# Closings of 14 row tiles: the residual rows added by an accumulating transfer, the post factor joined to the row factor

## The chip, the cores and the metric

One core of one Trainium2 chip runs the whole program. The metric is the device time of one execution in microseconds (us), the median of three executions. Engines are named as in the profile: PE (matmuls), DVE (VectorE), ACT (ScalarE), POOL (GpSimd), SP (the queue that issues most transfers).

## The reference

One decoder layer is applied to a prompt of 2048 rows and to a sample group of 32 rows. Four mixers (convolution, pooling, stick-breaking attention, cross-attention) give `mix`, 2048 values a row. What matters here is the end of the layer:

```python
out = rms_norm(mix @ w_out, post_g)     # y * rsqrt(mean(y*y) + eps) * post_g
xp = x + out
y_prompt = rms_norm(xp, final_g)
```

So every output row needs two row factors in turn: one from the sum of squares of the projection, one from the sum of squares of residual plus normalised projection. All of it is float32.

## The kernel before, in words

The program first does the input projections and the sample group's attention, then the prompt's attention, and at last the output projection `mix @ w_out`. That projection works on 16 row tiles of 128 rows and two halves of 512 columns. It is written as seven products for each pair of row tiles i (0 to 7), which are then combined by additions in two kept buffers, `U2` and `U3`. Products 1, 7, 2 and 6 run first, for all i. From position `last_` of the list `order` (L1915 to L1919) products 4, 5 and 3 follow, in the order (4,0) (4,1) (5,0) (5,1) (4,2) (5,2) (3,0) (3,1) (3,2), then the sample rows (5,8) (3,8), then for i = 3 to 7 each (4,i) (5,i) (3,i). This document calls that part the last stage. A product is 24 matmuls of 128x512 into one PSUM bank (tile `acc`). The eight banks are taken in turn: three of pool `accp`, five of `accp2` (L1962).

When a product is complete, `out_ready` adds the kept buffers to it on DVE (L1768, L1769), ACT takes its sum of squares (L1729, into `ssk`), DVE multiplies it by its half of `post_g` (L1772, in place in the bank), and the bank is held. Product 5 completes row tile t = 2i + 1, product 3 row tile t = 2i. The first half of an even tile was computed earlier and stored to DRAM; it comes back as tile `oh` (L1784), and POOL multiplies it by `post_g` (L1788, `out_factor`).

A complete row tile is closed by `out_tile`. The residual rows are loaded into tile `oxt` by SP (L1794; three buffers). DVE adds the two partial sums of squares (L1798), ACT takes the root (L1799), DVE the reciprocal (L1800). DVE then does one instruction per half, `xt = half * factor + xt` (L1804), and ACT squares each half with a sum (L1805). DVE, ACT and DVE make the second factor (L1808, L1809, L1810), DVE multiplies by it and by `final_g` (L1815), and SP stores the rows (L1817). The small tile `oss` that holds these factors has one buffer, so a closing begins only when the closing before it has done L1815. Tile 14 uses the other half of tile 15's buffer, so these two overlap.

PE runs in the order of the code. For DVE, ACT, POOL and SP a scheduler that works at build time chooses the order, and each of them then executes its list strictly in order. What feeds the last stage shares these lists: SP loads the rows of `mix` (`mr`, L1672, L1687), POOL adds two of them for product 5 (L1699), ACT rounds them (`mh`, L1714), DVE takes the remainder (`ml`, L1725), and PE multiplies (L1969).

Of the kernel before, what the change touches and what calls it, by code (L numbers as in the profile page):

```python
# [13 lines left out]
ALU = mybir.AluOpType  # L14
# [4 lines left out]
P = 128  # L19
# [68 lines left out]
def kernel(  # L88
# [9 lines left out]
    pe, act, dve, pool, sp = nc.tensor, nc.scalar, nc.vector, nc.gpsimd, nc.sync  # L98
    wq = nc.sync

    xp, xs = x_prompt[0], x_sample.rearrange("b t d -> (b t) d")
# [1625 lines left out]
    def square(c, t, half):  # L1727
        rows = P if t < 16 else NS
        act.activation(out=junk[:rows], in_=c[:rows], func=AF.Square, accum_out=ssk[:rows, t, half : half + 1])  # L1729

    def out_ready(prod, i, o):

        if i == LAST:
            if prod == 5:
                return
            both = (ope.tile([P, 512], F32, tag="oh", name="both3", bufs=OH) if prod == 3 else
                    op.tile([P, 512], F32, name=f"both{prod}", bufs=1))
            act.copy(both[:NS], o[NS : 2 * NS])
            dve.tensor_tensor(out=both[:NS], in0=both[:NS], in1=o[:NS], op=ALU.add)
            if prod == 1:  # L1740
                keep["s"] = both
            elif prod == 2:
                dve.tensor_tensor(out=both[:NS], in0=both[:NS], in1=keep["s"][:NS], op=ALU.add)
                square(both, 16, 0)
                keep[16, 0] = both
            else:
                dve.tensor_tensor(out=o[:NS], in0=both[:NS], in1=keep["s"][:NS], op=ALU.add)
                square(o, 16, 1)
                dve.tensor_tensor(out=o[:NS], in0=o[:NS], in1=gpost[:NS, 512:], op=ALU.mult)
                dve.tensor_tensor(out=keep[16, 0][:NS], in0=keep[16, 0][:NS], in1=gpost[:NS, :512], op=ALU.mult)  # L1750
                out_tile(16, keep[16, 0], o)
            return
        t = 2 * i + (prod in (4, 5))
        if prod == 1:
            act.copy(U2[:, i], o)
        elif prod == 7:
            dve.tensor_tensor(out=U3[:, i], in0=o, in1=U2[:, i], op=ALU.add)
        elif prod == 6:
            dve.tensor_tensor(out=U3[:, i], in0=o, in1=U3[:, i], op=ALU.add)
            dve.tensor_tensor(out=U2[:, i], in0=o, in1=U2[:, i], op=ALU.add)  # L1760
        elif prod == 2:
            c = opw.tile([P, 512], F32, tag="c11", name=f"c11_{i}", bufs=1)
            dve.tensor_tensor(out=c, in0=o, in1=U2[:, i], op=ALU.add)
            square(c, t, 0)
            sp.dma_start(c11d[i], c)
        else:
            if prod == 5:
                dve.tensor_tensor(out=U2[:, i], in0=o, in1=U2[:, i], op=ALU.add)  # L1768
            dve.tensor_tensor(out=o, in0=o, in1=(U2 if prod == 3 else U3)[:, i], op=ALU.add)  # L1769
            half = 0 if prod == 4 else 1  # L1770
            square(o, t, half)
            dve.tensor_tensor(out=o, in0=o, in1=gpost[:, 512 * half : 512 * half + 512], op=ALU.mult)  # L1772
            keep[t, half] = o
            if prod != 4:
                out_tile(t, keep[t, 0], keep[t, 1])
            if (prod, i) == (3, 0):
                out_first(2)
            if prod == 5 and i != 2 or (prod, i) == (3, 1):
                out_factor(2 if prod == 3 else i)

    def out_first(i):

        c = ope.tile([P, 512], F32, tag="oh", name=f"oh2_{i}", bufs=OH)
        sp.dma_start(c, c11d[i])  # L1784
        keep[2 * i, 0] = c

    def out_factor(i):
        pool.tensor_tensor(out=keep[2 * i, 0], in0=keep[2 * i, 0], in1=gpost[:, :512], op=ALU.mult)  # L1788

    def out_tile(t, a, b):  # L1790

        rows = P if t < 16 else NS
        xt = ope.tile([P, D], F32, tag="oxt", name=f"oxt{t}", bufs=OX)[:rows]
        sp.dma_start(xt, xp[P * t : P * t + P, :] if t < 16 else xs)  # L1794
        if t != 14:
            keep["ss"] = ope.tile([P, 6], F32, tag="oss", name=f"oss{t}", bufs=1)
        ss = keep["ss"][:rows, 3:] if t == 14 else keep["ss"][:rows]
        dve.tensor_tensor(out=ss[:, 0:1], in0=ssk[:rows, t, 0:1], in1=ssk[:rows, t, 1:2], op=ALU.add)  # L1798
        act.activation(out=ss[:, 0:1], in_=ss[:, 0:1], func=AF.Sqrt, bias=eps_t[:rows], scale=1.0 / D)  # L1799
        dve.reciprocal(out=ss[:, 0:1], in_=ss[:, 0:1])  # L1800
        last = t == 14
        halves = (slice(0, 512), slice(512, 1024))
        for n, (hs, src) in enumerate(zip(halves, (a[:rows], b[:rows]))):
            dve.scalar_tensor_tensor(out=xt[:, hs], in0=src, scalar=ss[:, 0:1], in1=xt[:, hs], op0=ALU.mult, op1=ALU.add)  # L1804
            act.activation(out=junk[:rows], in_=xt[:, hs], func=AF.Square, accum_out=ss[:, n + 1 : n + 2])  # L1805
        if last:
            keep.pop("end")()
        dve.tensor_tensor(out=ss[:, 1:2], in0=ss[:, 1:2], in1=ss[:, 2:3], op=ALU.add)  # L1808
        act.activation(out=ss[:, 1:2], in_=ss[:, 1:2], func=AF.Sqrt, bias=eps_t[:rows], scale=1.0 / D)  # L1809
        dve.reciprocal(out=ss[:, 1:2], in_=ss[:, 1:2])  # L1810
        dst = y_prompt[0, P * t : P * t + P, :] if t < 16 else y_sample.rearrange("b t d -> (b t) d")

        def end():
            for n, hs in enumerate(halves if last else (slice(0, 1024),)):
                dve.scalar_tensor_tensor(out=xt[:, hs], in0=xt[:, hs], scalar=ss[:, 1:2], in1=gfin[:rows, hs],  # L1815
                                         op0=ALU.mult, op1=ALU.mult)
                (wq if n else sp).dma_start(dst[:, hs], xt[:, hs])  # L1817

        if t == 15:
            keep["end"] = end  # L1820
        else:
            end()
# [186 lines left out]
    op = oy.enter_context(tc.tile_pool(name="op", bufs=1, side="right", reuse_waits="tile"))  # L2009
# [74 lines left out]
    for n, x in enumerate(parts):  # L2084
        if n == last_:
# [3 lines left out]
            gpost = ope.tile([P, D], F32, name="gpost", bufs=1)  # L2089
# [3 lines left out]
        prod, i, h = x  # L2093
# [20 lines left out]
        while done:  # L2114
            out_ready(*done.pop(0))
# [33 lines left out]
```

## Time and profile before

| | us |
|---|---|
| median of 3 executions | 2368.04 (2366.82 to 2369.79) |
| the profiled execution, its own time | 2371.25 |
| its span in the trace | 2369.5 |
| last stage, from its first loads to the last matmul | about 2212 to 2354.5 |
| from the last matmul to the end of the span | 15.0 |
| busy over the span: PE, DVE, ACT, POOL | 96%, 72%, 47%, 54% |

Rows of the timeline give start (us from the start of the span), duration (us), engine, line, operation, output and inputs. Rows that group instructions give the count behind an x and durations in ns. SPq is the issuing side of SP's queue; an issue is not the transfer, which goes on after it.

### The profile page before, as it was taken

The numbers are of one execution on the slowest core, as the hardware profiler recorded it, in microseconds if no ns is written. First come the engines' busy times: TensorE is split into PE (matmuls) and PEld (weight loads), VectorE is DVE, ScalarE is ACT, GpSimd is POOL, SyncE is SP. The second block draws the span as 40 slices with busy tenths as digits, with TensorE's granted clock in tenths as the row PEclk, the third lists the DMA queues.
The fourth block names the chain that finished last, engine by engine and source line by source line (L and its number), as shares of the span: only waits on it lengthen the run. The fifth ranks groups of instructions, "written<-read, shape, count | busy, mean of one in ns | idle before, by whom it ended". The sixth has DMA issues, their size and how long they took to land. (4 is left out here: it accounts for less than half of the span.)

```text
span 2369.5 us, 42238 instructions
## 1 busy us (share of the span) xinstructions
PE 2280.5 (96%) x16024; PEld 1775.3 (75%) x16024; DVE 1716.2 (72%) x2428; ACT 1117.2 (47%) x1947; POOL 1273.2 (54%) x1322
## 2 busy tenths in 40 slices
PE   7999999999999999999999999899999999989997
PEld 7998888898888777777777777555555557778775
DVE  5332696969747664577787868888897956777897
ACT  5322243242442322234242324798989965444554
POOL 3554545556474645545546463688988754432230
PEclk9999999999999999999999999999999999999998
DMA  6688977878778999987877775756534207766774
GB/s 206 198 268 282 344 270 258 287 251 287 245 261 313 308 356 332 328 282 263 303 265 257 275 268 151 175 167 173 164 115 114 76 26 248 260 207 200 237 247 150
DMA packets 336868, 557.94 MB, mean 235 GB/s; under 512 B 27985, under 2 KB 212433, under 8 KB 320266
## 3 DMA queue, kind: packets, MB, share of 16 engines
q1 hardware_dynamic: 281290, 286.53, 39.1%
q0 software_dynamic: 55376, 268.72, 32.1%
q8 instruction: 126, 2.06, 0.3%
q14 instruction: 76, 0.62, 0.1%
HBM read 465.09 MB, written 90.68 MB: 235 GB/s over the span
## 5 line engine op out<-in xcount | busy, mean ns | idle before, releaser
L966 DVE STREAM_TRANSPOSE T<-kt 128x1024 f32<-128x1024 f32 x256 | 308.6, 1226 | 192.5 <-PE sSA L979 178.9
L933 POOL DMA_INDIRECT vt<-in_cache_v_dram,idv x256 | 252.4, 986 | 257.1 <-PE sO L1018 196.0
L618 DVE SCALAR_TENSOR_TENSOR cacc<-U,par,cacc 128x512 f32<-128x512 f32 x480 | 359.7, 749 | 11.0
L1344 POOL TENSOR_TENSOR be<-be,E 128x512 f32<-128x512 f32 (+3 forms) x316 | 299.9, 961 | 59.8 <-DVE E L1335 25.8
L1335 DVE TENSOR_TENSOR_SCAN E<-gam,cr,ZM 128x513 f32<-128x513 f32 x192 | 232.7, 1262 | 14.6 <-ACT gam L1266 11.2
L933 POOL DMA_INDIRECT kt<-in_cache_k_dram,idk x128 | 128.1, 1001 | 197.3 <-DVE T L966 150.2
L1355 PEld LDWEIGHTS AT<-ident,be 128*128 128x128 f32 x1082 | 116.1, 141 | 128.9 <-ACT at L1361 48.2
L1969 PE MATMUL acc<-wohi,mh 128*128 128x512 f32 (+1 forms) x480 | 194.7, 406 | 1.6 <-ACT mh L1714 1.0
L1266 ACT ACTIVATE gam<-S,nbias_bc 128x1024 f32<-128x1024 f32 (+1 forms) x158 | 172.9, 1094 | 42.6 <-ACT be L1267 18.6
L1969 PE MATMUL acc<-wolo,mh 128*128 128x512 f32 (+1 forms) x480 | 190.8, 397 | 0.0
L1969 PE MATMUL acc<-wohi,ml 128*128 128x512 f32 x448 | 179.3, 400 | 8.1 <-DVE ml L1725 8.1
L1262 PE MATMUL S<-kT,Q 128*128 128x512 f32 (+1 forms) x632 | 173.5, 397 | 4.9 <-ACT be L1267 4.8
L1267 ACT ACTIVATE be<-S,bias_bc 128x1024 f32<-128x1024 f32 (+1 forms) x158 | 171.7, 1087 | 0.9 <-DMA gsd<-sg1sg 0.9
L1355 PE MATMUL AT<-ident,be 128*128 128x128 f32 x1082 | 157.5, 283 | 13.9 <-DVE at L1359 7.4
L1371 PE MATMUL av<-at,V 128*64 128x512 f32 (+3 forms) x640 | 152.8, 556 | 3.5 <-DVE sbo L1376 3.5
L979 PE MATMUL sSA<-T,W 128*32 128x128 f32 x4096 | 140.5, 276 | 3.3 <-DVE T L966 1.4
L979 PEld LDWEIGHTS sSA<-T,W 128*32 128x32 f32 x4096 | 105.3, 109 | 38.5 <-issue 31.5
L1018 PE MATMUL sO<-vt,saT 128*32 128x512 f32 x1024 | 122.1, 592 | 0.0
L1262 PEld LDWEIGHTS S<-kT,Q 128*128 128x128 f32 x632 | 104.5, 192 | 18.5 <-ACT be L1267 6.3
L1361 ACT COPY at<-AT 128x512 f32<-128x512 f32 x192 | 110.9, 677 | 12.2 <-PE AT L1355 12.2
L1332 DVE TENSOR_TENSOR_SCAN E<-gam,ZM 128x384 f32<-128x384 f32 (+1 forms) x124 | 94.3, 809 | 28.6 <-ACT gam L1266 23.5
L1725 DVE TENSOR_TENSOR ml<-mr,mh 128x512 fp32r<-128x512 f32 x108 | 86.6, 808 | 33.5 <-ACT mh L1714 33.3
(577 smaller groups left out, 6036.2 us busy)
## 6 DMA issues: line engine op xcount, KB each, us to landing
Q<-qd SPq DMA_DIRECT2D x64, 256.0 KB
mr<-mixd SPq DMA_DIRECT2D x32, 512.0 KB
mr<-mixd SPq DMA_DIRECT2D x48, 256.0 KB
xtp<-in_x_prompt_dram SPq DMA_DIRECT2D x16, 512.0 KB
kT<-kd SPq DMA_DIRECT2D x64, 128.0 KB
ws<-in_w_out_dram SPq DMA_DIRECT2D x16, 512.0 KB
wsd<-ws SPq DMA_DIRECT2D x16, 512.0 KB
msd<-mr SPq DMA_DIRECT2D x32, 256.0 KB
```

Source lines behind the costliest of these rows:

```text
L618: dve.scalar_tensor_tensor(out=ps, in0=U[:, a + k : a + k + H], scalar=wd[:, k : k + 1], in1=ps, op0=ALU.mult, op1=ALU.add)
L933: pool.indirect_dma_start(out=dst, out_offset=None, in_=rows, in_offset=bass.IndirectOffsetOnAxis(ap=idx, axis=0))
L966: S["turn"] = dve.transpose(T[:, 2 * hh : 2 * hh + 2].rearrange("p s j t -> p (s j t)"), kt[:, 2 * hh : 2 * hh + 2].rearrange("p s j d -> ...
L979: pe.matmul(sSs[n][32 * g : 32 * g + 32, P * ml : P * (ml + 1)], lhsT=W[:, jj, :], rhs=T[:, :, jj, :], start=i == 0, stop=i == 3, tile_pos ...
L1262: pe.matmul(S[:, j, :w], lhsT=Q[:, x, P * (q2 + j) : P * (q2 + j + 1)], rhs=kt[:, :w], start=x == 0, stop=x == 1)
L1266: act.activation(out=ga, in_=S[:, :, :w], func=AF.Sigmoid, bias=nbias_bc[:, h : h + 1], scale=-1.0)
L1267: act.activation(out=be, in_=S[:, :, :w], func=AF.Sigmoid, bias=bias_bc[:, h : h + 1])
L1335: dve.tensor_tensor_scan(out=E[:, j][:, ::-1], data0=g_[:, j][:, ::-1], data1=ZM[:, 0:1].to_broadcast([P, 513]), initial=carry[hh, q2][:, ...
L1344: newest.append(pool.tensor_tensor(out=be[:, j, :m], in0=be[:, j, :m], in1=E[:, j, 513 - w : 513 - w + m], op=ALU.mult).ins)
L1355: pe.transpose(ap_[:, P * qt : P * (qt + 1)], A[hp, qb, kc, hh, qt][:, P * r : P * (r + 1)], ident)
L1371: pe.matmul(av[64 * hh : 64 * hh + 64, c], lhsT=V[:, 4 * kc + r, 64 * hh : 64 * hh + 64], rhs=ats.pop((hp, qb, kc, r, hh))[:, c], start=dg ...
L1969: pe.matmul(o[:rows], lhsT=m[a][:, k, :rows], rhs=W[prod, 4 * h + k][w], start=not cont and h == k == n == 0, stop=h == 1 and k == 3 and n ...
```

## The change

For the 14 row tiles t = 0 to 13:

- L1772 (multiplication of a finished half by `post_g` on DVE) and L1788 (the same for `oh` on POOL) are left out. Only the three halves of tiles 14 and 15 that pass L1772, and the one L1788 for tile 14, remain.
- L1804 becomes `xt = half * factor * post_g`, which writes `oxt` and no longer reads it (L1811 in the changed kernel).
- The load of the residual rows by SP goes away. In its place POOL issues a transfer that reads the same rows from DRAM and adds them to `oxt` (L1814). It waits for both L1811, and both squares of ACT (now L1816) wait for it.

Tiles 14, 15 and the sample tile 16 are closed as before.

```diff
@@ out_ready
             square(o, t, half)
-            dve.tensor_tensor(out=o, in0=o, in1=gpost[:, 512 * half : 512 * half + 512], op=ALU.mult)
+            if t > 13:
+                dve.tensor_tensor(out=o, in0=o, in1=gpost[:, 512 * half : 512 * half + 512], op=ALU.mult)
             keep[t, half] = o
...
-            if prod == 5 and i != 2 or (prod, i) == (3, 1):
-                out_factor(2 if prod == 3 else i)
+            if (prod, i) == (5, 7):
+                out_factor(i)
@@ out_tile
-        sp.dma_start(xt, xp[P * t : P * t + P, :] if t < 16 else xs)
+        x_rows = xp[P * t : P * t + P, :] if t < 16 else xs
+        if t > 13:
+            sp.dma_start(xt, x_rows)
...
-        for n, (hs, src) in enumerate(zip(halves, (a[:rows], b[:rows]))):
-            dve.scalar_tensor_tensor(out=xt[:, hs], in0=src, scalar=ss[:, 0:1], in1=xt[:, hs], op0=ALU.mult, op1=ALU.add)
+        for hs, src in zip(halves, (a[:rows], b[:rows])):
+            if t > 13:
+                dve.scalar_tensor_tensor(out=xt[:, hs], in0=src, scalar=ss[:, 0:1], in1=xt[:, hs], op0=ALU.mult,
+                                         op1=ALU.add)
+            else:
+                dve.scalar_tensor_tensor(out=xt[:, hs], in0=src, scalar=ss[:, 0:1], in1=gpost[:, hs], op0=ALU.mult,
+                                         op1=ALU.mult)
+        if t < 14:
+            pool.dma_start(out=xt, in_=x_rows, accum_op=ALU.add)
+        for n, hs in enumerate(halves):
             act.activation(out=junk[:rows], in_=xt[:, hs], func=AF.Square, accum_out=ss[:, n + 1 : n + 2])
```

The scheduler gives the four engines other orders with this change. On DVE, near the end of the program, these rows stood around the last two products. A name holds the product or tile number and then i: `acc5_7` is the bank of product (5,7), `oss12` and `oxt12` are the factors and rows of tile 12.

```order
L1798 TENSOR_TENSOR oss12_23882<-ssk_20132 128x1
L1769 TENSOR_TENSOR acc4_7_23904<-acc4_7_23904,U3_20131 128x512
L1800 RECIPROCAL oss12_23882<-oss12_23882 128x1
L1725 TENSOR_TENSOR ml3_7_1_23955<-mr3_7_1_23895,mh3_7_1_23954 128x512
L1804 SCALAR_TENSOR_TENSOR oxt12_23880<-oh2_6_23748,oss12_23882,oxt12_23880 128x512
L1804 SCALAR_TENSOR_TENSOR oxt12_23880<-acc3_6_23843,oss12_23882,oxt12_23880 128x512
L1808 TENSOR_TENSOR oss12_23882<-oss12_23882 128x1
L1772 TENSOR_TENSOR acc4_7_23904<-acc4_7_23904,gpost_22691 128x512
L1810 RECIPROCAL oss12_23882<-oss12_23882 128x1
L1815 SCALAR_TENSOR_TENSOR oxt12_23880<-oxt12_23880,oss12_23882,gfin_22692 128x1024
L1768 TENSOR_TENSOR U2_20130<-acc5_7_23940,U2_20130 128x512
```

In the changed kernel DVE's list has these rows around the addition of product (5,7) (L1768) and of product (3,7) (the last L1769):

```order
L1819 TENSOR_TENSOR oss8_23556<-oss8_23556 128x1
L1768 TENSOR_TENSOR U2_20130<-acc5_7_23912,U2_20130 128x512
L1821 RECIPROCAL oss8_23556<-oss8_23556 128x1
L1769 TENSOR_TENSOR acc5_7_23912<-acc5_7_23912,U3_20131 128x512
L1826 SCALAR_TENSOR_TENSOR oxt8_23555<-oxt8_23555,oss8_23556,gfin_22692 128x1024
L1801 TENSOR_TENSOR oss11_23651<-ssk_20132 128x1
L1803 RECIPROCAL oss11_23651<-oss11_23651 128x1
L1811 SCALAR_TENSOR_TENSOR oxt11_23650<-acc4_5_23578,oss11_23651,gpost_22691 128x512
L1811 SCALAR_TENSOR_TENSOR oxt11_23650<-acc5_5_23617,oss11_23651,gpost_22691 128x512
L1819 TENSOR_TENSOR oss11_23651<-oss11_23651 128x1
L1769 TENSOR_TENSOR acc3_7_23960<-acc3_7_23960,U2_20130 128x512
L1801 TENSOR_TENSOR oss10_23704<-ssk_20132 128x1
```

(Between the last L1819 and the last L1769 stand only L1821 and L1826 of tile 11.) Before, all closings up to tile 12 had ended ahead of the addition of (5,7). Now tile 8 is still open there, tile 11 follows, and tiles 10, 13, 12, 15 and 14 stand behind the addition of (3,7), the last product.

POOL's list now holds the 14 accumulating transfers among its additions for product 5 (`mr4_...` is the slot that products 4 and 5 share; `oxt7` is the transfer of tile 7). Around i = 7 it reads:

```order
L1699 TENSOR_TENSOR mr4_7_0_23740<-mr4_7_0_23740 128x512
L1814 DMA oxt7_23354<-in_x_prompt_dram 128x1024
L1699 TENSOR_TENSOR mr4_7_1_23760<-mr4_7_1_23760 128x512
L1814 DMA oxt6_23407<-in_x_prompt_dram 128x1024
L1814 DMA oxt9_23502<-in_x_prompt_dram 128x1024
L1814 DMA oxt8_23555<-in_x_prompt_dram 128x1024
```

Before, no transfer stood in that part of POOL's list. The last addition for product 5 now stands behind the transfer of tile 7, and the seven transfers of tiles 6, 9, 8, 11, 10, 13 and 12 follow it.

On ACT the two squares of a closing are now one piece, behind the casts that the scheduler had put between or after them. For tile 1 the list before read:

```order
L1714 CAST mh5_2_1_22959<-mr4_2_1_22797 128x512
L1805 ACTIVATE junk_20133,oss1_22851<-oxt1_22849 128x512 x2
L1729 ACTIVATE junk_20133,ssk_20132<-acc5_1_22868 128x512
L1809 ACTIVATE oss1_22851<-oss1_22851,eps_t_93 128x1
L1714 CAST mh3_0_0_22984<-mr3_0_0_22888 128x512
L1714 CAST mh3_0_1_23007<-mr3_0_1_22933 128x512
```

and now reads:

```order
L1714 CAST mh5_2_1_22953<-mr4_2_1_22795 128x512
L1714 CAST mh3_0_0_22977<-mr3_0_0_22884 128x512
L1816 ACTIVATE junk_20133,oss1_22847<-oxt1_22846 128x512 x2
L1729 ACTIVATE junk_20133,ssk_20132<-acc5_1_22864 128x512
L1820 ACTIVATE oss1_22847<-oss1_22847,eps_t_93 128x1
L1714 CAST mh3_0_1_23000<-mr3_0_1_22927 128x512
```

The cast for (3,0) moved ahead of the squares of tile 1; the cast for its second half stays behind them, and behind the wait that they now have.

## The prediction

> **What bounds the kernel now.** I read first the busy time by engine in windows of the last stage, since only that stage changes. Columns: window, length, then busy time and count of PE, PEld, DVE, ACT and POOL, the granted clock, the DMA share and GB/s.
>
> ```profile
> 2212.00:2354.50 142.50, 138.60 (x594) 109.86 (x592) 125.98 (x222) 72.69 (x193) 28.87 (x20) 0.99 0.63 216
> 2354.50:2369.50 15.00, 0.02 (x1) 0.00 (x0) 8.40 (x18) 5.29 (x16) 0.00 (x0) 0.57 0.23 92
> 2302.00:2316.00 14.00, 14.00 (x62) 11.40 (x61) 13.50 (x22) 5.89 (x16) 5.31 (x3) 1.00 0.65 236
> PE acc L1969 <- DVE ml L1725: 3.3, 3, 2.4
> ```
>
> PE is busy for 138.6 of 142.5 us, DVE for 126.0; behind the last matmul lies a tail of 15 us without PE. The fourth row, from the waits of PE in the stage, says that PE waited 3.3 us for DVE. So the stage is PE's, with DVE close behind. A full window holds 62 matmuls in 14 us, so a product of 24 takes 24 x 14/62 = 5.4 us.
>
> The chain that ended last has 16 pieces, and its first is this one:
>
> ```profile
> 2361.72 0.09 issue
> ```
>
> It reaches back only into the closing of tile 14, so I follow the closings by DVE's timeline: where the first begins, how one waits for PE, the sample tile's slot, and all of tile 15's.
>
> ```profile
> 2232.65 0.15 DVE L1798 TENSOR_TENSOR oss<-ssk 128x1 f32<-128x1 f32 x1
> ...
> 2281.28 0.14 DVE L1798 TENSOR_TENSOR oss<-ssk 32x1 f32<-32x1 f32 x1
> ...
> 2288.88 0.14 DVE L1798 TENSOR_TENSOR oss<-ssk 128x1 f32<-128x1 f32 x1
> ...
> 2336.64 1.34 DVE L1815 SCALAR_TENSOR_TENSOR oxt<-oxt,oss,gfin 128x1024 f32<-128x1024 f32 x1
> 2337.90 0.68 DVE L1769 TENSOR_TENSOR acc<-acc,U 128x512 f32<-128x512 f32 x1
> 2340.31 0.14 DVE L1798 TENSOR_TENSOR oss<-ssk 128x1 f32<-128x1 f32 x1
> ...
> 2355.80 0.15 DVE L1798 TENSOR_TENSOR oss<-ssk 128x1 f32<-128x1 f32 x1
> 2356.30 0.16 DVE L1800 RECIPROCAL oss<-oss 128x1 f32<-128x1 f32 x1 [0.36 <-ACT oss L1799]
> 2356.50 1.41 DVE L1804 SCALAR_TENSOR_TENSOR oxt<-acc,oss,oxt 128x512 f32<-128x512 f32 x2
> ...
> 2360.17 0.15 DVE L1810 RECIPROCAL oss<-oss 128x1 f32<-128x1 f32 x1
> 2360.24 0.14 DVE L1798 TENSOR_TENSOR oss<-ssk 128x1 f32<-128x1 f32 x1
> 2360.36 1.28 DVE L1815 SCALAR_TENSOR_TENSOR oxt<-oxt,oss,gfin 128x1024 f32<-128x1024 f32 x1
> ```
>
> From 2232.65 (tile 1) to 2355.80 (tile 15) there are 15 closings, 8.2 us apart; tile 10's ends at 2337.98 and tile 13's begins 2.3 us later, after PE's product. So the closings keep up with PE with little to spare. They are strictly one after the other, because `oss` has one buffer. That is where this change acts.
>
> **Part one, what goes.** Fewer instructions on DVE and POOL, 14 loads off SP.
>
> ```profile
> L1772 DVE TENSOR_TENSOR acc<-acc,gpost x24: 668/699/700, 2223.7 to 2359.6; 128x512 f32<-128x512 f32 x24
> L1788 POOL TENSOR_TENSOR oh<-oh,gpost x8: 1286/1292/2223, 2220.7 to 2335.6; 128x512 f32<-128x512 f32 x8
> L1804 DVE SCALAR_TENSOR_TENSOR oxt<-acc,oss,oxt x25: 729/743/752, 2234.4 to 2362.5; 128x512 f32<-128x512 f32 x24, 32x512 f32<-32x512 f32 x1
> ```
>
> 21 of the 24 instructions of L1772 go, 21 x 0.70 = 14.7 us of DVE, and 7 x 1.29 = 9.0 us of POOL. The fused instruction has two inputs from the same kinds of memory as L1804, so I keep its 0.74 us (bounds 0.7 and 0.75, the two DVE rows above). The saving is hidden behind PE: PE waited 3.3 us for DVE in all, and that is the most that it can return there. In the tail it returns nothing, as the three halves of tiles 14 and 15 keep L1772. SP's 14 issues stood behind no one who waits.
>
> **Part two, what one closing becomes.** Both squares now wait for the transfer, and the transfer for both fused instructions; the single `oss` makes every later closing wait as well. I take tile 15's rows above and ACT's rows of the same closing:
>
> ```profile
> 2357.34 0.63 ACT L1805 ACTIVATE junk<-oxt 128x512 bf16<-128x512 f32 x1 [1.06 <-DVE oxt L1804]
> ...
> 2358.62 0.19 ACT L1805 ACTIVATION_READ_ACCUMULATOR junk<-oxt 128x1 f32 x1
> 2358.84 0.60 ACT L1729 ACTIVATE junk<-acc 128x512 bf16<-128x512 f32 x1
> ...
> 2359.43 0.28 ACT L1809 ACTIVATE oss<-oss,eps_t 128x1 f32<-128x1 f32 x1
> ```
>
> - L1798 to the first L1804: 2356.50 - 2355.80 = 0.70
> - both fused instructions: 1.41
> - POOL's issue: 0.87 (row below)
> - landing of the transfer, from the end of the issue: L
> - both squares, 2357.34 to 2358.81: 1.47 (before, the first lay beside the second L1804)
> - the square of a later product, then the second root, 2358.81 to 2359.71: 0.90
> - reciprocal 0.19 and L1815 1.28: 1.47
>
> That is 6.8 us + L. The changed order puts on the way of most closings one more DVE instruction of about 0.7 us (a remainder or an addition between a closing's end and the next one's start, or ahead of the fused pair); I add 0.8, and call that an estimate. One closing: 7.6 + L.
>
> **L is not in the trace**, since no transfer there accumulates. The nearest rows:
>
> ```profile
> 2338.01 0.34 SPq L1817 DMA_DIRECT2D out_dram<-oxt  x1
> 2340.68 0.33 SPq L1794 DMA_DIRECT2D oxt<-in_x_prompt_dram  x1
> ...
> 133.07 1.22 POOL L933 DMA_INDIRECT kt<-in_cache_k_dram,idk  x1 [3.48 <-DVE idk L865]
> 139.30 1.25 DVE L966 STREAM_TRANSPOSE T<-kt 128x1024 f32<-128x1024 f32 x1 [4.95 <-DMA kt<-in_cache_k_dram,idk]
> ...
> 1953.97 0.87 POOL L1377 DMA_DIRECT2D mixd<-sbo  x1 [21.83 <-DVE sbo L1376]
> ```
>
> (1) A plain transfer of 512 KB by SP, with nothing beside it: issue ends at 2338.35, the load that waits for its buffer goes out at 2340.68: 2.3 us. (2) POOL's gather of 1 MB with a quiet DMA: issue ends at 134.29, its reader starts at 139.30: 5.0 us. (3) POOL's one direct transfer, 256 KB on loaded DMA engines: issue ends at 1954.84, and its first packets appear in the half microsecond from 1957.5, 2.7 us later, where the gather's first came within 0.7. The DMA view of three windows of half a microsecond says so (packets, MB, share of 16 engines): SP's queue from 1954.5, POOL's from 1957.5, and POOL's at the gather from 134.5:
>
> ```profile
> q1 hardware_dynamic: 87, 0.18, 92.1%
> ...
> q0 software_dynamic: 9, 0.04, 17.9%
> ...
> q0 software_dynamic: 1, 0.01, 6.2%
> ```
>
> An accumulation of 512 KB reads two sources, 1 MB, and goes through POOL's queue, so (2) is the nearest row: **L = 5.0 us**. Lower bound 2.3 (1). Upper bound 3.0 + 5.0 = 8.0 (the late start of (3) and then the time of (2)). Below 2.3 I see no reason: it moves more than (1). The removed load was off the path, so nothing is gained against L.
>
> The Trainium skill, page "DMA: Bandwidth & Descriptors", section "Anatomy of one DMA — SWDGE (gpsimd) path", fits a transfer of this queue as 2.0 us plus bytes over 436 GB/s; an estimate by it is 3.2 us for 512 KB, and the sum below would be 25 us smaller. The gather of 1 MB agrees roughly with that fit (4.4 us by it, 5.0 in the trace), and no run here shows an accumulation yet.
>
> **The sum.** A closing takes 7.6 + 5.0 = 12.6 us; PE delivers two row tiles in three products, 3 x 5.4 = 16.2 us, so 8.1 us for each. From the first closing on the chain of closings is the bound, and PE waits for banks, which the closings hold. 14 closings x 12.6 = 176.4; the sample tile's slot stays at 2288.88 - 2281.28 = 7.6; from tile 15's start to the end of the span it stays 2369.5 - 2355.8 = 13.7. 2232.65 + 176.4 + 7.6 + 13.7 = 2430.4, against a span of 2369.5: **+61 us**. The profiled execution took 2371.25 and would take 2432; the median of the runs shown lies 3.2 us under it, so I predict **2429**.
>
> What waits behind the new wait: on ACT the casts `mh` of coming products stand behind the squares, so up to 6 us late; on POOL the additions for product 5 stand behind a transfer that waits for DVE. PE waits for both, but the products that they feed are needed only one closing later, and the chain has by then taken 12.6 us; I cost them at nothing as long as the chain is the bound. SP issues the loads for tiles 15 and 14 behind the store of tile 13, and tile 12's closing covers them. If PE were the bound, each late cast would cost up to 6 us.
>
> **Rivals.**
>
> (a) *PE stays the bound, with a short landing.* At L = 2.3 a closing takes 9.9, near PE's 8.1, and the order decides: the rows of DVE's list show tile 11's closing behind the addition of (5,7), and five closings behind that of (3,7). (3,7) needs a bank of tile 11. (5,7) ends about 5.4 us before 2354.5, at 2349.1; additions, reciprocal, L1826, and tile 11's start up to its first fused instruction take about 4.1 (3 x 0.6 + 1.3 + 1.0); (3,7) starts near 2353.9 and ends near 2359, tile 11 ends near 2361.5, then come three closings of 9.1 (without the 0.8) and 13.7: about 2402, +33 us, 2401. For it: the plain row. Against it: the gather's row.
>
> (b) *The transfer lands late.* At L = 8.0 the sum grows by 14 x 3.0 = 42: 2471. For it: the late start of POOL's direct transfer. Against it: the DMA share was then near 1, and here it is 0.63 and falls as the stage stretches.
>
> (c) *The wait is hidden and DVE's saving shows.* This ends on the other side. PE gets back its 3.3 us and the tail is as before: 2365. It decides where a closing stays under PE's 8.1 us, that is L under 0.5 us, and only if the last five closings did not stand behind (3,7). Both rows and the order speak against it.
>
> That the change doesn't do what it says is excluded on the side of DVE: its list has 1900 rows in place of 1921, the 21 that go.
>
> **How the numbers follow.** The forecast (chain of closings, L from 3.5 to 6.5: 2408 to 2450) gets 0.58, (a) 0.15, (b) 0.24, (c) 0.03. The range takes in (a) and (b) as the bounds of L: 2401 to 2471. Faster or slower count from 0.2%, 4.7 us, about what a measurement of this kernel can tell from no change: faster 0.02, within it 0.01, slower 0.97. No case between the landing's lower bound and (c) gives a time near the old one.
>
> **What would show it.** In the changed profile: ACT's squares L1816 wait for the transfer about 5 us after POOL's issue, 14 times; the fused rows at 0.74 us; closings about 12.6 us apart; PE idle for some 20 us of the last stage, in waits for banks that DVE releases; five closings behind the last matmul, so a tail of about 55 us in place of 15 (the rest of tile 11's closing, three of 12.6, and 13.7). The forecast is wrong if closings are under 10 us apart, if PE's waits go to casts or to additions of POOL rather than to banks, or if the tail holds fewer than five closings.

## The result and the profile after

The changed kernel takes **2440.1 us** (median of 5 runs, 2436.0 to 2443.8) against 2368.0 us before on the same chip: **1.0305 times the time before (95% interval 1.0287 to 1.0322), 72 us more**. The forecast was 2429, in a range of 2401 to 2471. The profiled execution also took 2440.1 us, with a span of 2438.4.

Busy time by window, first up to 2.3 us behind the last matmul and then to the end (columns as in the prediction):

```profile
2212.00:2383.00 171.00, 143.55 (x579) 110.75 (x578) 95.39 (x173) 64.24 (x164) 25.77 (x23) 0.92 0.54 147
2383.00:2438.40 55.40, 0.00 (x0) 0.00 (x0) 19.19 (x41) 13.62 (x42) 3.83 (x4) 0.51 0.39 109
```

PE's share of the stage falls from 138.6 of 142.5 us to 143.6 of 171 (its granted clock falls from 0.99 to 0.92), and 55 us follow in which no engine is busy even half of the time. When every engine idles, the bound is a chain with waits in it. The waits from 2212 us on name its links (engine, line, who released it: us in total, times, longest); the last four are all that PE has:

```profile
POOL oxt L1814 <- DVE oxt L1811: 119.3, 13, 12.1
ACT junk L1816 <- DMA oxt<-in_x_prompt_dram: 92.3, 14, 11.0
DVE oss L1819 <- ACT junk L1816: 89.1, 17, 10.9
...
PE acc L1980 <- DVE oxt L1811: 12.8, 2, 6.5
PE acc L1980 <- DVE mh L1725: 6.3, 1, 6.3
PE acc L1980 <- ACT mh L1714: 4.7, 4, 3.2
...
PE acc L1980 <- DVE ml L1725: 1.4, 3, 0.9
```

Read from top to bottom they are a ring: POOL waits for DVE's scaling, ACT's squares wait for POOL's transfer, DVE's next step waits for the squares, and DVE's next scaling, for which POOL waits again, stands behind that. One turn of it is the closing of tile 10, behind the last matmul (DVE, ACT and POOL rows in order of time; the last row is the next closing's first):

```profile
2383.78 0.15 DVE L1801 TENSOR_TENSOR oss<-ssk 128x1 f32<-128x1 f32 x1
...
2384.49 0.75 DVE L1811 SCALAR_TENSOR_TENSOR oxt<-oh,oss,gpost 128x512 f32<-128x512 f32 x1
2385.16 0.75 DVE L1811 SCALAR_TENSOR_TENSOR oxt<-acc,oss,gpost 128x512 f32<-128x512 f32 x1
...
2386.43 0.84 POOL L1814 DMA_DIRECT2D oxt<-in_x_prompt_dram  x1 [11.88 <-DVE oxt L1811]
...
2392.07 0.63 ACT L1816 ACTIVATE junk<-oxt 128x512 bf16<-128x512 f32 x1 [7.82 <-DMA oxt<-in_x_prompt_dram]
...
2393.58 0.16 DVE L1819 TENSOR_TENSOR oss<-oss 128x1 f32<-128x1 f32 x1 [7.68 <-ACT junk L1816]
...
2394.68 1.28 DVE L1826 SCALAR_TENSOR_TENSOR oxt<-oxt,oss,gfin 128x1024 f32<-128x1024 f32 x1
...
2396.07 0.16 DVE L1801 TENSOR_TENSOR oss<-ssk 128x1 f32<-128x1 f32 x1
```

Of the 12.3 us of this closing, 6.16 lie between the end of the second L1811 (2385.91) and the squares (2392.07): 0.52 until POOL starts the issue, 0.84 of issue, 4.80 of landing. The first row of the first closing, the last matmul, and the first row of tile 15's closing are:

```profile
2227.70 0.16 DVE L1801 TENSOR_TENSOR oss<-ssk 128x1 f32<-128x1 f32 x1 [0.23 <-ACT junk L1729]
...
2380.29 0.40 PE L1980 MATMUL acc<-wohi,ml 128*128 128x512 f32 x1
...
2424.72 0.16 DVE L1801 TENSOR_TENSOR oss<-ssk 128x1 f32<-128x1 f32 x1
```

All 14 transfers in one row group, and its landing counted from the start of the issue:

```profile
L1814 POOL DMA_DIRECT2D oxt<-in_x_prompt_dram x14: 835/854/927, 2231.2 to 2411.0; - x14
...
DMA to landing us min/median/max: 5.4/5.6/8.8
```

### The profile page after: what moved, and what is told of

The parts are those of the page before. It is cut to its first block, busy times and chain, and to the rows that moved or that the text cites. A ratio compares the mean times of both kernels' runs of the same rounds, so it can differ in the third digit from the quotient of the medians.

```text
span 2438.4 us, 42229 instructions
## 1 busy us (share of the span) xinstructions
PE 2282.0 (94%) x16024; PEld 1773.2 (73%) x16024; DVE 1701.2 (70%) x2407; ACT 1118.2 (46%) x1947; POOL 1275.4 (52%) x1329
## 5 line engine op out<-in xcount | busy, mean ns | idle before, releaser
L1980 PE MATMUL acc<-wohi,mh 128*128 128x512 f32 (+1 forms) x480 | 197.8, 412 | 24.8 <-DVE oxt L1811 12.8
L1355 PE MATMUL AT<-ident,be 128*128 128x128 f32 x1082 | 156.9, 282 | 15.7 <-DVE at L1359 8.6
L1980 PEld LDWEIGHTS acc<-wohi,mh 128*128 128x128 f32 (+1 forms) x480 | 91.2, 190 | 49.5 <-ACT mh L1714 14.5
L1361 ACT COPY at<-AT 128x512 f32<-128x512 f32 x192 | 111.0, 678 | 12.2 <-PE AT L1355 12.2
```

What stands on the lines that cost most here:

```text
L1355: pe.transpose(ap_[:, P * qt : P * (qt + 1)], A[hp, qb, kc, hh, qt][:, P * r : P * (r + 1)], ident)
L1980: pe.matmul(o[:rows], lhsT=m[a][:, k, :rows], rhs=W[prod, 4 * h + k][w], start=not cont and h == k == n == 0, stop=h == 1 and k == 3 and n ...
```

## The experiments

The theory after the result: a transfer that is issued only when the scaled rows are ready, and whose landing the closing waits for, puts its whole landing on the chain 14 times, and nothing else runs beside it. What keeps other work from running beside it was open: the single `oss` buffer (as the prediction had it) or the order in which ACT and DVE work through their lists. The rival: the transfer itself costs bandwidth or slows other transfers, so that hiding it would not help. Each run is a median with the kernel before on the same chip beside it (2367.2 to 2369.1 us).

### Factor columns of each tile's own

```diff
-            keep["ss"] = ope.tile([P, 6], F32, tag="oss", name=f"oss{t}", bufs=1)
+            keep["ss"] = qsT.rearrange("p c t -> p (c t)")[:, 6 * t : 6 * t + 6]
```

(`qsT` is a tile that nothing uses any more in this stage.) In the changed kernel:

> The changed kernel, but each row tile has factor columns of its own (slices of a dead tile) in place of the single buffer oss. Theory A of the prediction (the single buffer is what keeps closings one after the other): closings overlap, PE is the bound again, 2370 to 2385 us. Theory B (ACT's list keeps them apart: the square of the next product, L1729, stands in code order behind the two squares that wait for the transfer): only the end of a closing, from the second root to L1826, gets beside the next one's start, about 2 us of 12.6 for each of 14: 2410 to 2420 us, closings about 10.7 us apart.

and the same edit in the kernel before:

> The kernel before with the same factor columns of its own: what the edit of e1 is worth without the transfer. Both theories: PE is the bound there, within 5 us of 2368.

Measured: 2436.5 us (2434.9 to 2439.0), ratio 1.029 (1.026 to 1.032), for the changed kernel, and 2368.8 us, ratio 1.000 (0.999 to 1.002), for the one before. Both sizes missed. The single buffer is worth at most some 4 us of the 72 (the ranges of the two kernels overlap); it is not what holds the closings apart. The lists are, since closing t+1 starts behind closing t in them. The trace of the first run, from DVE's last addition to a product to the start of tile 12's closing:

```profile
2385.35 0.69 DVE L1769 TENSOR_TENSOR acc<-acc,U 128x512 f32<-128x512 f32 x1
...
2391.50 0.63 ACT L1816 ACTIVATE junk<-oxt 128x512 bf16<-128x512 f32 x1 [8.76 <-DMA oxt<-in_x_prompt_dram]
...
2393.01 0.60 ACT L1729 ACTIVATE junk<-acc 128x512 bf16<-128x512 f32 x1
2393.01 0.16 DVE L1819 TENSOR_TENSOR qsT<-qsT 128x1 f32<-128x1 f32 x1 [6.97 <-ACT junk L1816]
...
2393.78 0.59 ACT L1729 ACTIVATE junk<-acc 128x512 bf16<-128x512 f32 x1
...
2394.11 1.28 DVE L1826 SCALAR_TENSOR_TENSOR oxt<-oxt,qsT,gfin 128x1024 f32<-128x1024 f32 x1
...
2395.31 0.15 DVE L1801 TENSOR_TENSOR qsT<-ssk 128x1 f32<-128x1 f32 x1
...
2403.43 0.63 ACT L1816 ACTIVATE junk<-oxt 128x512 bf16<-128x512 f32 x1 [7.64 <-DMA oxt<-in_x_prompt_dram]
...
2404.94 0.60 ACT L1729 ACTIVATE junk<-acc 128x512 bf16<-128x512 f32 x1
...
2405.66 0.16 DVE L1801 TENSOR_TENSOR qsT<-ssk 128x1 f32<-128x1 f32 x1 [0.56 <-ACT junk L1729]
```

L1801 of tile 13 no longer waits for a buffer, yet DVE reaches it only at 2395.31, behind L1819 and L1826 of tile 10, which waited for tile 10's transfer. ACT's list holds it back almost as long: L1801 adds two sums that L1729 makes, and the two L1729 at 2393.01 and 2393.78, tile 13's by count (one follows for each later product), stand behind tile 10's squares. The addition ends at 2386.04, so by then every product is ready to be squared, and these rows wait for nothing but their place in the list. At tile 12 the profile names this wait itself: 0.56 us for the L1729 behind tile 13's squares. So theory B (the lists) named the right cause. Its size, about 2 us for each closing, was too large: the 14 closings together take 184.3 us in place of 190.0, and the first of them begins 2.3 us later.

### The transfer without the joined instruction

L1772 and L1788 come back, and L1811 only multiplies by the row factor; the transfer stays.

```diff
-            if t > 13:
-                dve.tensor_tensor(out=o, in0=o, in1=gpost[...], op=ALU.mult)
+            dve.tensor_tensor(out=o, in0=o, in1=gpost[...], op=ALU.mult)
...
-                dve.scalar_tensor_tensor(out=xt[:, hs], in0=src, scalar=ss[:, 0:1], in1=gpost[:, hs], ...)
+                dve.tensor_scalar(out=xt[:, hs], in0=src, scalar1=ss[:, 0:1], scalar2=None, op0=ALU.mult)
```

> The accumulating transfer alone: L1772 and L1788 are back for all tiles, L1811 becomes half times row factor. If the whole loss is the transfer in the chain of closings: 2435 to 2450, closings 12.6 us apart in the tail, as in the changed kernel, since the 14.7 us of DVE that come back stand beside the landing. If the joined instruction had given much of its DVE time back on the path: 2450 or more.

Measured: 2453.9 us (2451.7 to 2458.2), ratio 1.037 (1.034 to 1.040). The transfer alone costs 85 us, which is the upper of the two expected cases, and the joined instruction gives back 14 of them. That this is close to its 14.7 us of DVE is in part chance. The two profiled spans differ by 15.7 us: 7.7 of these lie in the 14 closings, 1.3 in the sample tile's slot, and 6.8 ahead of the first closing, which begins at 2234.46 in place of 2227.70. So with PE no longer the bound some of that DVE work lies on the chain, about half of it by these two executions.

### Two transfers of 256 KB, each behind its half

```diff
-        if t < 14:
-            pool.dma_start(out=xt, in_=x_rows, accum_op=ALU.add)
+                pool.dma_start(out=xt[:, hs], in_=x_rows[:, hs], accum_op=ALU.add)
```

> The changed kernel with two transfers of 256 KB per tile, each issued behind its own half of L1811. If the landing scales in part with bytes and the halves overlap: the first square hides behind the second landing (0.75 us) and the second landing is about 0.6 us shorter, so 12.6 becomes about 11.3 and the time about 2420. If each transfer costs its full landing in turn on POOL's queue: closings of 15 us or more, 2470 or more.

Measured: 2437.8 us (2434.7 to 2440.5), ratio 1.029 (1.026 to 1.032). Neither expected case came. The last two of the 14 closings, which lie behind the last matmul, are shorter (10.85 us in place of 12.22, and 13.56 in place of 16.43); the twelve ahead of them take 161.8 us together in place of 161.4, and the last matmul ends 12.8 us later. Its waits of PE (from 2212 us on) are other ones than in the changed kernel, 30 us for the casts and remainders of the next products and none for a bank:

```profile
PE acc L1979 <- ACT mh L1714: 17.4, 8, 4.2
PE acc L1979 <- DVE ml L1725: 8.0, 10, 2.2
PE acc L1979 <- DVE mh L1725: 4.7, 2, 3.6
```

The casts stand on ACT among squares that now wait twice per closing. Whether that order alone moved the last matmul was not tried.

### A plain transfer in the same place, on POOL's queue and on SP's

The transfer overwrites the tile instead of adding to it, first from POOL, then from SP:

```diff
-            pool.dma_start(out=xt, in_=x_rows, accum_op=ALU.add)
+            pool.dma_start(out=xt, in_=x_rows)
```

> The changed kernel, with the 14 transfers left on GpSimd's queue but without the accumulation (they overwrite the tile, so tiles 0 to 13 leave out the normalised projection). Theory A, the addition makes the landing long: start of the issue to the squares falls from 5.6 us (median in the changed kernel) to about 4.4, closings are 1.2 us shorter, and the time is 2440 - 14 x 1.2 = about 2423 us (2418 to 2430). Theory B, GpSimd's queue itself is the price and the addition is free: 5.4 to 5.7 us again and 2435 to 2443 us.

```diff
-            pool.dma_start(out=xt, in_=x_rows, accum_op=ALU.add)
+            sp.dma_start(out=xt, in_=x_rows)
```

> The changed kernel, with the 14 transfers issued by SyncE at the same place and without the accumulation (they overwrite the tile, so tiles 0 to 13 leave out the normalised projection). If a closing is 7.6 us plus the landing, as predicted, and SyncE's transfer of 512 KB lands in 2.3 to 3.0 us after its issue as its residual loads did in the kernel before, then each closing is 2.0 to 2.7 us shorter and the time is 2440 - 14 x 2.0 to 2.7 = 2402 to 2412 us. If GpSimd's issue and queue are not what a closing waits for: 2430 us or more.

Measured: 2416.0 us (ratio 1.020, 1.018 to 1.023) on POOL's queue and 2407.3 us (1.017, 1.015 to 1.020) on SP's. On POOL, a group row and the landing from the start of the issue (the profiled execution took 2425.0 us, the longest of the four; its first closing begins 5.5 us later than in the changed kernel):

```profile
L1814 POOL DMA_DIRECT2D oxt<-in_x_prompt_dram x14: 531/536/589, 2236.7 to 2397.5; - x14
...
DMA to landing us min/median/max: 3.8/4.1/7.1
```

On SP, the scaling, the issue and the squares of one closing with no other load beside it:

```profile
2368.55 1.41 DVE L1811 SCALAR_TENSOR_TENSOR oxt<-acc,oss,gpost 128x512 f32<-128x512 f32 x2
2370.03 0.33 SPq L1814 DMA_DIRECT2D oxt<-in_x_prompt_dram  x1
2373.76 0.63 ACT L1816 ACTIVATE junk<-oxt 128x512 bf16<-128x512 f32 x1 [5.44 <-DMA oxt<-in_x_prompt_dram]
```

From the start of the issue a plain transfer lands in 4.1 us and an accumulating one in 5.6: theory A. 14 x 1.5 = 21 us of the 24 between the two kernels, and the 14 closings take 169.3 us in place of 190.0. From the end of the scaling (2369.96) SP's squares come after 3.80 us, against 6.16 in the changed kernel. So even the faster of the two plain ways to bring 512 KB at this place leaves the kernel 40 us slower than before: most of the loss is neither POOL's queue nor the addition, but that the transfer begins so late.

### The squares one closing later

Everything behind the transfer (squares, second root, L1826, store) is written behind the scaling of the next tile, for tiles 0 to 13, with factor columns of each tile's own:

```diff
+        def late():
             for n, hs in enumerate(halves):
                 act.activation(out=junk[:rows], in_=xt[:, hs], func=AF.Square, accum_out=ss[:, n + 1 : n + 2])
...
+        for f in keep.pop("late", ()):
+            f()
+        if t < 14:
+            keep["late"] = late, end
+            return
+        late()
```

In the changed kernel, and as a control in the kernel before:

> The changed kernel with factor columns of each tile's own, and with the part of a closing that stands behind the transfer (squares, root, last scaling, store) written one closing later for tiles 0 to 13. Theory A, the in-order lists of ScalarE and VectorE hold everything up behind squares that wait for a landing: with the next tile's work written ahead of those squares the landing of 5.6 us lies beside it, closings come 8 us apart again as TensorE gives their banks, and the time is 2360 to 2375 us. Theory B, the transfers themselves are the limit (they slow each other and the loads on the shared DMA engines): the landings grow with the overlap, and the time is 2400 to 2435 us.

> The control for the run with the squares written later: the kernel before (residual rows loaded by SyncE, no accumulation) with the same two edits. Its loads are there when the closing begins, so writing the squares one closing later should hide nothing: 2363 to 2373 us by both theories. A time under 2360 us would say that the order alone is worth something, and what the run beside it gains would then be put down to the order and not to the hidden landing; a time over 2378 us that the later squares cost something of their own.

Measured: **2374.2 us** (median of 12 runs, ratio 1.003, 1.002 to 1.005), and for the control 2362.1 us (12 runs, ratio 0.998, 0.996 to 0.999). The same 14 accumulating transfers, with a median landing of 6.2 us, now leave the kernel 7 us slower than before in place of 72; against the joined instruction without any transfer (2359.6 us, below) they cost 14.6 us in place of 80.5. Two closings of this kernel, from the first scaling (the profiled execution took 2385.2 us, the longest of the 12):

```profile
2300.09 1.41 DVE L1811 SCALAR_TENSOR_TENSOR oxt<-acc,qsT,gpost 128x512 f32<-128x512 f32 x2
2301.80 0.86 POOL L1814 DMA_DIRECT2D oxt<-in_x_prompt_dram  x1 [6.12 <-DVE oxt L1811]
2302.92 0.16 DVE L1801 TENSOR_TENSOR qsT<-ssk 128x1 f32<-128x1 f32 x1 [0.22 <-ACT junk L1729]
...
2306.44 0.85 POOL L1814 DMA_DIRECT2D oxt<-in_x_prompt_dram  x1 [1.51 <-DVE oxt L1811]
2307.46 0.64 ACT L1817 ACTIVATE junk<-oxt 128x512 bf16<-128x512 f32 x1 [3.54 <-DMA oxt<-in_x_prompt_dram]
```

The transfer goes out at 2301.80, DVE takes up the next tile at 2302.92, and the squares that need the first transfer come at 2307.46, behind the second tile's issue. ACT still waits 25.1 us for landings in all (92.3 in the changed kernel); a closing in this order comes at times 5 us behind the one before it, less than the landing. The closings are not the 8 us apart that theory A named, but mostly about 5 and 9 to 14 in turn. Theory B is out: overlapped, the transfers land in 6.2 us in place of 5.6 (medians). Of the control's gain of 5 us I had expected none, so the order alone is worth a little; with it, the kernel without accumulating transfers is 12 us faster than with them, and it is the fastest complete version of this study, 0.2% under the kernel before.

### The last two loads left out

```diff
-        if t > 13:
+        if t > 15:
             sp.dma_start(xt, x_rows)
...
-                dve.scalar_tensor_tensor(..., in1=xt[:, hs], op0=ALU.mult, op1=ALU.add)
+                dve.scalar_tensor_tensor(..., in1=(xt if t == 16 else gpost)[:rows, hs], op0=ALU.mult, op1=ALU.add)
```

> The changed kernel without the two SyncE loads of the residual rows of tiles 15 and 14 (those two tiles add the post factor's row in place of their residual rows). Theory A, these loads share the DMA engines with the accumulating transfer of tile 12 and make it late: its squares come 5.4 to 5.8 us after the start of its issue, in place of 8.9, the other thirteen as before, and the time is 2440 - 3.2 = about 2437 us (2434 to 2439). Theory B, that landing is late for a reason of its own (its place as the last transfer of GpSimd's queue): over 8 us again, and 2438 to 2443 us.

Measured: 2434.9 us (2433.5 to 2438.9), ratio 1.029 (1.027 to 1.030). Tile 12 in the changed kernel, whose transfer has both loads of SP beside it:

```profile
2408.78 2.82 SPq L1797 DMA_DIRECT2D oxt<-in_x_prompt_dram  x2
...
2410.96 0.86 POOL L1814 DMA_DIRECT2D oxt<-in_x_prompt_dram  x1 [11.35 <-DVE oxt L1811]
2419.82 0.63 ACT L1816 ACTIVATE junk<-oxt 128x512 bf16<-128x512 f32 x1 [11.04 <-DMA oxt<-in_x_prompt_dram]
```

and without them:

```profile
2412.64 0.86 POOL L1814 DMA_DIRECT2D oxt<-in_x_prompt_dram  x1 [11.22 <-DVE oxt L1811]
2418.46 0.63 ACT L1816 ACTIVATE junk<-oxt 128x512 bf16<-128x512 f32 x1 [8.01 <-DMA oxt<-in_x_prompt_dram]
```

8.86 us become 5.82: theory A, some 3 us of the 72. (The time fell by 5.2; the other 2 are within the spread of the runs.)

### The joined instruction without the transfer

```diff
-        if t < 14:
-            pool.dma_start(out=xt, in_=x_rows, accum_op=ALU.add)
```

and, as its control, the kernel before with the 14 residual loads left out, the final factor's row being added in their place:

```diff
-        sp.dma_start(xt, xp[P * t : P * t + P, :] if t < 16 else xs)
+        if t > 13:
+            sp.dma_start(xt, xp[P * t : P * t + P, :] if t < 16 else xs)
...
-            dve.scalar_tensor_tensor(..., in1=xt[:, hs], op0=ALU.mult, op1=ALU.add)
+            dve.scalar_tensor_tensor(..., in1=(xt if t > 13 else gfin)[:rows, hs], op0=ALU.mult, op1=ALU.add)
```

> The joined instruction without the transfer: the changed kernel with the 14 accumulating transfers left out (tiles 0 to 13 leave out the residual rows). As the prediction had part one, its 14.7 us of VectorE lie behind TensorE and at most 3.3 us come back: 2364 to 2370 us. By a line through the three runs with different landings (2407, 2416 and 2440 us at 3.8, 4.65 and 6.2 us from the end of the joined instruction to the squares, 13.9 us for each us of landing) the closings would end 14 x 6.2 us sooner than in the changed kernel, at 2354 us (2350 to 2360), with TensorE not the bound.

> The control for the joined instruction alone: the kernel before with the 14 residual loads left out (tiles 0 to 13 add the row of the final factor in place of their residual rows, with the same instruction). If the loads are hidden as the prediction had it: 2365 to 2371 us. If they cost something by their share of the DMA engines or by the wait for a buffer: under 2363 us, and the joined instruction alone is then to be held against this time and not against 2368.

Measured: 2359.6 us (2356.4 to 2364.1), ratio 0.997 (0.995 to 0.998), and 2367.3 us for the control, ratio 1.000 (0.999 to 1.001). The loads that the change removes cost nothing before; the joined instruction by itself gains 7.7 us. That is more than the 3.3 of the prediction, and inside the lower of the two expected ranges (2350 to 2360), though not for its reason: PE is the bound, busy 131.9 of 132.5 us up to its last matmul. That last matmul and the first row of tile 15's closing, with the joined instruction:

```profile
2343.99 0.40 PE L1978 MATMUL acc<-wohi,ml 128*128 128x512 f32 x1
2344.49 0.15 DVE L1801 TENSOR_TENSOR oss<-ssk 128x1 f32<-128x1 f32 x1
```

and without it:

```profile
2346.75 0.40 PE L1970 MATMUL acc<-wohi,ml 128*128 128x512 f32 x1
...
2349.94 0.15 DVE L1799 TENSOR_TENSOR oss<-ssk 128x1 f32<-128x1 f32 x1
```

Without it DVE has a backlog when PE ends, and tile 15's closing begins 3.2 us behind the start of the last matmul in place of 0.5. So 2.7 us come from the tail and 2.8 from PE's end, which together are the 5.4 us by which the two profiled spans differ.

## Why the prediction was right, and where it was off

The runs in which one thing at a time is added give the ladder of the loss:

| kernel | us | step |
|---|---|---|
| before, its 14 loads left out | 2367.3 | |
| joined instruction, no transfer | 2359.6 | -7.7 |
| with a plain transfer by SP behind the scaling | 2407.3 | +47.7 |
| the same by POOL | 2416.0 | +8.7 |
| accumulating (the change) | 2440.1 | +24.1 |
| the same with the squares one closing later and own factors | 2374.2 | -65.9 |

By the prediction's own steps:

- **The chain of closings becomes the bound: right, and shown.** Hiding the landing without removing a single transfer takes back 66 of the 72 us; the order that does it gives the kernel before 5 us as well, so some 61 are the landing's.
- **What makes it a chain: wrong in part.** "They are strictly one after the other, because `oss` has one buffer" was argued from the code. A buffer for each tile takes back at most some 4 us; the closings follow one another because DVE and ACT work through lists in which the next closing's first rows stand behind rows that wait for the landing. The sum was not touched by this, since both give the same chain.
- **One closing, 12.6 us: right for the undisturbed ones.** Nine of the 14 take 12.2 to 13.1 us, 12.7 in the mean. L was put at 5.0; the clean landing is 4.8 from the end of the issue, close to the row of the gather. The 0.52 us ahead of the issue, which the sum did not have, is in these closings about taken up by the 0.8 of extra DVE work; that the two agree so well is luck, since the 0.8 stood for something else. **The Trainium skill**, "DMA: Bandwidth & Descriptors", section "Anatomy of one DMA — SWDGE (gpsimd) path", gave 3.2 us as an estimate. The plain transfer of this queue agrees roughly (4.1 less 0.54 of issue is 3.6); for the accumulating one the trace says 4.8, and the trace decides.
- **The term that was mis-sized: 14 closings at 12.6 = 176.4 us measured 190.0** (first rows of the closings from 2227.70 to 2424.72, less 7.0 of the sample tile). The excess of 13.6 us is nearly all in five closings, which take 13.9, 14.2, 14.8, 16.6 and 16.4 us. Its parts are two. The landing holds 4.5 us of it: counted from the start of the issue, where the sum had 5.87, four landings take 6.5, 6.9, 7.7 and 8.9 us, and the ten others 5.66 in the mean. The other 9 us lie on either side of the landing, in steps that the sum put at 6.75 us (5.95 from rows and the 0.8) and that measure 7.4 us in the mean.
- **What made these five longer.** Of the four late landings the last, tile 12's, is shown: "tile 12's closing covers them" was wrong, since SP's two loads slow that transfer by 3.0 us. In the three others SP's queue moved 1.22, 1.29 and 1.59 MB while they were under way, at most 0.77 MB in any of the ten that were on time; that this is the cause is argued by likeness and was not tried. Outside the landings, the first closing holds a table load of ACT (ACT_TABLE_LOAD on L1802, 1.28 us from 2227.68), two others have an L1826 of 1.76 and 1.82 us in place of 1.28, which begin while a POOL addition is running, and the two longest, tile 12's among them, have two DVE rows of 0.7 us for other work between the squares and their L1826. What these are worth was not tried either.
- **The rest of the sum.** First closing 2227.70 in place of 2232.65, 5 us early, which is luck: no term of the sum stood for it, and the run with plain transfers on POOL's queue, whose kernel differs only in those transfers, had it at 2233.24; tile 15 to the end 2438.4 - 2424.7 = 13.7, as predicted. 13.6 - 5.0 - 0.6 of the sample tile's slot = 8.0, the difference of the spans 2438.4 and 2430.4; 3 more lie in the profiled execution of before, which was 3 us over its median where that of after was on it.
- **Joined instruction, at most 3.3 us and nothing in the tail: too little.** Alone it gains 7.7 us, because DVE's backlog in the tail goes as well. In the changed kernel it returns 14, as the cover that was named for it (PE as the bound) is gone; about half of that was found in the closings. The prediction's sum used the shorter instruction list in the closing but never counted this return.
- **PE's waits.** Predicted some 20 us for banks; measured 25.2 in all, 12.8 for banks and 12.4 for casts and remainders. Half of them are thus of the kind that the prediction named as a sign against itself. The casts were thus not free on PE. That the chain covered these waits, as the prediction had it, is argued; no run takes them away alone.
- **The tail: right.** Five closings behind the last matmul; 2438.4 - 2380.7 = 57.7 us against 55.
- **The rivals.** (a), a short landing, gave 2402 for the plain row's 2.3 us; the run with a plain transfer by SP took 2407 at 3.4 us from the end of the issue, with its last matmul ending at 2355.9 where (a) had 2359. So (a)'s path is near that of a plain transfer by SP, a landing that the accumulating one does not have. (b) needed 8 us in every closing, and one of 14 had it. (c) needed something to hide the wait; the run with the squares later shows that another order does most of that, which the change did not bring.

## What to carry to other kernels

Before a load is replaced by a transfer that adds in place, ask when it can start: the load could begin long before its reader, the accumulating transfer only behind the last write of its target, so its whole landing goes to whatever reads the target next. An instruction that waits for a landing also holds everything behind it in its engine's list, so write at least one landing's worth of other work between the issue and the first reader, or leave the load early. A saving on an engine that is nearly the bound also counts behind the bounding engine's last instruction, where its backlog is worked off.

## What the runs showed of the hardware

An accumulating transfer of 512 KB on GpSimd's queue costs more than a plain one of the same shape on the same queue: 0.85 against 0.54 us of issue, and 5.6 against 4.1 us from the start of the issue to the reader (medians of 14). The profile counts its 0.52 MB once, but in a microsecond in which the accumulating transfer has the DMA engines to itself they are as good as full (0.97) at 193 GB/s, and the plain one moves 283 GB/s at 0.70 of them. One microsecond of each, from the middle of a transfer, first the changed kernel and then the plain transfer (the last two columns are the DMA share and GB/s):

```profile
2390.00:2391.00 1.00, 0.00 (x0) 0.00 (x0) 0.00 (x0) 0.00 (x0) 0.00 (x0) 0.50 0.97 193
```

```profile
2389.00:2390.00 1.00, 0.00 (x0) 0.00 (x0) 0.00 (x0) 0.00 (x0) 0.00 (x0) 0.50 0.70 283
```

Per engine share that is 199 against 404 GB/s, about a half, as if each byte passed twice; the profile does not show the second pass.
